# Mixer heads in halves of TensorE's rows or columns, in place of zero-filled operands

## The chip, the cores and the metric

One core of a Trainium2 chip runs the whole program. The metric is the device time of one execution in microseconds (us), the median of three runs. TensorE (PE) multiplies; VectorE (DVE) and ScalarE (ACT) do the elementwise work; SyncE (SP) issues the loads of weights.

## The reference, cut to what is computed

```python
for l in range(2):                      # h: 272 tokens (16 meta + 256) x 1024
    h += 0.5 * swiglu(rms(h), ffn1)     # 1024 -> 2816 -> 1024
    p = rms(h) @ w_in                   # 2688 columns, split over three head groups
    A = hgrn2(q, f, v, g)               # 6 heads of 64: gated linear recurrence, rms per head, gate
    B = sliding_window(q, k, v, sinks)  # 6 query heads, 2 key heads of 64, window 128, meta tokens
    C = conformer_conv(u)               # 256 channels, 31 taps, LayerNorm, swish
    h += concat(A, B, C) @ w_out
    h += 0.5 * swiglu(rms(h), ffn2)
return rms(h[:, 16:])
```

## The kernel before

Activations lie with channels on the 128 partitions and the 272 tokens along the free axis. Weights stream from HBM in 1 MB chunks; `Weights.split` makes of each a high part (ACT, L114) and a residual (DVE, L116), and every 128x128 weight tile is multiplied in three fp32r matmuls (L230 to L232). The fp32 matmuls of the mixer are run by the chip in two passes each, every pass with its own weight load.

A mixer is a row of projections, `proj(name, between, ...)`: 24 weight matmuls and then the small jobs in `between`, in the program's order on PE. ACT and DVE take theirs in an order that a scheduler writes down at build time. The jobs that the change touches:

- Recurrence (group A): the causal 272x272 matrix of each of 6 heads is built in levels b = 1, 2, 4, ... 64. `pairs(b)` multiplies keys `kk` (two heads of 64 channels share a 128-row tile) with the odd blocks of the queries. `stage(b)` copies those blocks into `qs`, per head into a half of its own, with the other head's rows zero: so one matmul over 128 rows gives both heads side by side, 128 columns wide (L470, and 16 wide for the last 16 tokens, L474). `keep(b)` copies the wanted places out of PSUM into `a0`, `a1`, `at`. `far` does the same for tokens 128 on (`ptl` L547, `pf` L552, from the zero-filled `qt` and `qs`).
- `outputs(i)`: values times matrix for the two heads of tile i, one after the other, three matmuls each (L601, L602, L603), head 0 into PSUM rows 0 to 63 and head 1 into 64 to 127. DVE adds the diagonal (L604), ACT squares (L605).
- `out_stats`: mean squares of the 6 heads with a 128x6 operand (`pr`, L611), root on ACT, reciprocal on DVE (L614). `out_norm(i)`: a 6x128 matmul spreads tile i's two factors over the partitions (`prb`, L618), one after each of three groups of output weights (`pw`); DVE multiplies (L619, L620) and splits into `y0h`, `y0l`.
- Attention (group B): `scores` puts a bf16 mask into PSUM (L659) and adds queries times keys (L661) per head; `bk` holds each key head with the other's rows zero. Then maximum (DVE L666), exp (ACT L671), normalisation (ACT L685, DVE L683), transposes (L697), and `values` (L729), in two column halves, one per key head.

Of the kernel before, what the change touches and what calls it, by code (L numbers as in the profile page):

```python
# [15 lines left out]
P = 128  # L16
# [121 lines left out]
def tile_hybrid_trunk(ctx: ExitStack, tc: tile.TileContext, hT: bass.AP, wst: bass.AP, par: bass.AP,  # L138
# [49 lines left out]
    for b in range(2):  # L188
        nc.gpsimd.memset(ones_q[b * 64:(b + 1) * 64, b * 64:(b + 1) * 64], 1.0)
    ident = cn[:, K_ID:K_ID + P]  # L190
# [166 lines left out]
    def mixer(l, nrm, t0, nxt):  # L357
# [16 lines left out]
        a0, a1, at = T([P, 6, N], "a0"), T([P, 6, 144], "a1"), T([META, 6, META], "at")  # L374
        qs = [T([P, 3, 2, 144], f"qs{i}") for i in range(2)]
        qt = T([P, 3, 2, META], "qt")
# [3 lines left out]
        bk = T([P, 2, N], "bk")  # L380
        for z in ([q[:, :, :t0]] if t0 else []) + [hc[:, :, :TAPS - 1], qs[0], qs[1], qt, bk, a0, a1, at]:
            nc.gpsimd.memset(z, 0.0)
# [73 lines left out]
        def stage(b):  # L456
            no = (N if b <= 8 else SEQ) // 2
            st = qs[levels.index(b) % 2]
            for hh in range(2):
                hs = slice(hh * 64, (hh + 1) * 64)  # L460
                nc.scalar.copy(st[hs, :, hh, :no].rearrange("p h (m b) -> p h m b", b=b),
                               odd(q[hs, :, :2 * no], b))

        def pairs(b):
            st = qs[levels.index(b) % 2]
            for g in range(2):
                ps = lev_ps[g] = bank(f"pl{b}_{g}_{l}")
                m = P if b < 64 else 64
                for i in range(3):
                    nc.tensor.matmul(ps[:m, i * P:(i + 1) * P], kk[:, i, g * P:g * P + m],  # L470
                                     st[:, i, :, g * 64:(g + 1) * 64], start=True, stop=True)
                if g == 1 and b <= 8:
                    for i in range(3):
                        nc.tensor.matmul(ps[:META, 384 + i * 16:384 + (i + 1) * 16], kk[:, i, SEQ:],  # L474
                                         st[:, i, :, 128:136], start=True, stop=True)

        def keep(b):
            lev = levels.index(b)
            for g, dst in enumerate((a0, a1)):
                ps = lev_ps[g]  # L480
# [13 lines left out]
            if b <= 8:  # L494
                shp = [META, 6, 8 // b, b]
                nc.vector.copy_predicated(
                    odd(at, b),
                    lv[:META, lev, :8].rearrange("p (m b) -> p m b", b=b).unsqueeze(1).broadcast_to(shp),
                    ps[:META, 384:432].rearrange("p (h m b) -> p h m b", h=6, b=b))
# [34 lines left out]
        def stage_far():  # L534
            tl = decay[128]
            st = qs[1]
            for hh in range(2):
                hs = slice(hh * 64, (hh + 1) * 64)
                nc.scalar.copy(qt[hs, :, hh, :], q[hs, :, SEQ:])
                nc.scalar.copy(st[hs, :, hh, :128], q[hs, :, 128:SEQ])  # L540
                nc.vector.tensor_tensor(st[hs, :, hh, 128:144], q[hs, :, SEQ:],
                                        tl[hs, :, 1:2].broadcast_to([64, 3, META]), op=ALU.mult)

        def far():
            ps = bank(f"ptl_{l}")
            for i in range(3):
                nc.tensor.matmul(ps[:, i * 32:(i + 1) * 32], kk[:, i, 128:SEQ],  # L547
                                 qt[:, i, :, :], start=True, stop=True)
            nc.scalar.copy(a1[:, :, 128:144], ps[:, :96].rearrange("p (h t) -> p h t", h=6))
            for i in range(3):  # L550
                ps = bank(f"pf{i}_{l}")
                nc.tensor.matmul(ps[:, :288], kk[:, i, :P], qs[1][:, i, :, :], start=True, stop=True)  # L552
                nc.scalar.copy(a0[:, 2 * i:2 * i + 2, 128:272],
                               ps[:, :288].rearrange("p (h t) -> p h t", h=2))
# [40 lines left out]
        def outputs(i):  # L595
            ps = bank(f"po{i}_{l}")
            for hh in range(2):
                hd = 2 * i + hh
                po = ps[hh * 64:(hh + 1) * 64, :]
                cs = slice(hd * 64, (hd + 1) * 64)  # L600
                nc.tensor.matmul(po[:, :N], vt[:, 0, cs], a0[:, hd, :], start=True, stop=False)  # L601
                nc.tensor.matmul(po[:, 128:272], vt[:, 1, cs], a1[:, hd, :], start=False, stop=False)  # L602
                nc.tensor.matmul(po[:, 256:272], vtt[:, cs], at[:, hd, :], start=False, stop=True)  # L603
            nc.vector.tensor_tensor(DG()[:, i, :], ps[:, :N], DG()[:, i, :], op=ALU.add)  # L604
            nc.scalar.activation(v[:, i, :], DG()[:, i, :], AF.Square)  # L605

        
        def out_stats():
            ps = bank(f"pr_{l}")
            for i in range(3):  # L610
                nc.tensor.matmul(ps[:6, :N], cn[:, K_B6 + 6 * i:K_B6 + 6 * i + 6], v[:, i, :], start=i == 0, stop=i == 2)  # L611
            rs = L([P, N], "rs", "rs")[:6, :]
            nc.scalar.activation(rs, ps[:6, :N], AF.Sqrt, bias=eps[:6])
            nc.vector.reciprocal(rs, rs)  # L614

        def out_norm(i):
            ps = bank(f"prb{i}_{l}")
            nc.tensor.matmul(ps[:, :N], cn[:6, K_S6 + i * P:K_S6 + (i + 1) * P], late["rs"][:6, :], start=True, stop=True)  # L618
# [12 lines left out]
        def keys(ps):  # L631
            for hh in range(2):
                hs = slice(hh * 64, (hh + 1) * 64)
                nc.vector.tensor_tensor(bk[hs, hh, :], ps[hs, :], r[hs, :], op=ALU.mult)

        class Heads:
# [3 lines left out]
            def __init__(self, name, groups, parts, lhs, prt, mask, nsk, kv):  # L640
                self.name, self.groups, self.parts, self.lhs, self.prt = name, groups, parts, lhs, prt
                self.mask, self.nsk, self.kv = mask, nsk, kv
                self.nk = sum(e - s for s, e in parts)
                self.per = 512 // self.nk
# [5 lines left out]
            def scores(self, g0):  # L650
                prt, nk = self.prt, self.nk
                ps = bank(f"ps{self.name}{g0}_{l}")
                g1 = min(self.groups, g0 + self.per)
                o = 0
                for gi in range(g0, g1):
                    mo = self.mask
                    for ks, ke in self.parts:
                        w = ke - ks
                        nc.tensor.matmul(ps[:prt, o:o + w], identb[:, :prt], conb[:, mo:mo + w],  # L659
                                         start=True, stop=False)  # L660
                        nc.tensor.matmul(ps[:prt, o:o + w], self.lhs(gi), bk[:, self.kv(gi), ks:ke],  # L661
                                         start=False, stop=True)
                        o += w
                        mo += w
                nm, nsk = self.nm[:, g0:g1], self.nsk[:prt, g0:g1]
                nc.vector.tensor_reduce(nm, ps[:prt, :o].rearrange("p (g k) -> p g k", g=g1 - g0),  # L666
                                        axis=AX.X, op=ALU.max)
                nc.vector.scalar_tensor_tensor(nm, nm, -SCALE, nsk, op0=ALU.mult, op1=ALU.min)
                for gi in range(g0, g1):
                    o = (gi - g0) * nk  # L670
                    nc.scalar.activation(self.p[:, gi, :], ps[:prt, o:o + nk], AF.Exp,  # L671
                                         bias=self.nm[:, gi:gi + 1], scale=SCALE,
                                         accum_out=self.den[:, gi:gi + 1])
# [29 lines left out]
        h0 = Heads("0", 6, [(0, 128)], lambda g: BQ()[:, g % 3, :P], P, K_M0, nsink[:, sk:sk + 6], lambda g: g // 3)  # L703
        h1 = Heads("1", 6, [(0, 256)], lambda g: BQ()[:, g % 3, P:SEQ], P, K_M1, nsink[:, sk:sk + 6], lambda g: g // 3)
        ht = Heads("t", 2, [(0, META), (P, N)], lambda g: bqt, 48, K_MT, nsinkt[:, 2 * l:2 * l + 2], lambda g: g)
# [16 lines left out]
        def values(hd, parts, sl):  # L722
            def go():
                ps = bank(f"pv{hd.name}_{l}")
                w = hd.groups * hd.prt // 2
                for kvh in range(2):
                    hs = slice(kvh * 64, (kvh + 1) * 64)
                    for pi, (off, kn, vsrc) in enumerate(parts):
                        nc.tensor.matmul(ps[hs, :w], vsrc[:kn, hs], pt[hd.name, off][:kn, kvh * w:(kvh + 1) * w],  # L729
                                         start=pi == 0, stop=pi == len(parts) - 1)  # L730
# [48 lines left out]
        proj("bv", [level(8, 1), lambda: h0.scores(0), lambda: h0.scores(4), lambda: h1.scores(0)], scaled(bv))  # L779
        proj("v0", [level(16, 1), bv_rows, lambda: h1.scores(2), lambda: h1.scores(4), h0.soft], scaled(v[:, 0, :]))  # L780
# [166 lines left out]
```

## Time and profile before

| | |
|---|---|
| median of 3 runs (lowest to highest) | 1061.64 us (1060.98 to 1061.72) |
| the profiled execution: time, span | 1060.9 us, 1059.1 us |
| TensorE's granted clock, whole span | 0.997 of full speed |
| busy share of the span: PE, DVE, ACT | 98%, 70%, 53% |
| mixer of layer 0, of layer 1 (by the places of their instructions) | about 212 to 338 us, 737 to 864 us |

A busy share counts overlapping instructions once. PE's matmuls are pipelined and their ends modelled, so a busy PE may still contain gaps, and the time of a small job is read from start to start, as the chain of waits gives it, and not from the duration of its instructions. All places below are in the mixer of layer 0; layer 1 repeats them.

### The profile page before, as it was taken

How to read it: one execution, taken by the hardware profiler on the slowest of the kernel's cores; microseconds unless marked ns; L12 is line 12 of the kernel's file. 1: busy time of each engine (PE TensorE's matmuls, PEld its weight loads, DVE VectorE, ACT ScalarE, POOL GpSimd, SP SyncE). 2: the span in 40 equal slices, each digit the busy share in tenths (PEclk: the TensorE clock that was granted, in tenths of full speed). 3: DMA queues.
4: the chain of work that ended last, by engine and by line, in shares of the span. 5: the costliest groups of instructions: out<-in, count | busy, mean ns of one | idle time of the engine just before them, and what ended most of it. 6: DMA issues, size and time to landing. Idle time of an engine off the chain costs nothing.

```text
span 1059.1 us, 19879 instructions
## 1 busy us (share of the span) xinstructions
PE 1043.0 (98%) x8324; PEld 1020.2 (96%) x8324; DVE 746.6 (70%) x1225; ACT 557.4 (53%) x879; POOL 13.1 (1%) x33
## 2 busy tenths in 40 slices
PE   7999999999999999999999999999999999999996
PEld 7999999999879999999999999999998799999996
DVE  7876655589968777665566766555999688767552
ACT  7644444454847644444454444444668466554441
POOL 0000000110000000000000000001000000000000
PEclk9999999999999999999999999999999999999998
DMA  8554554554214454544545454454422245545521
GB/s 313 223 189 168 178 180 166 194 176 151 79 52 152 168 199 160 189 169 174 185 162 195 162 182 178 162 187 169 174 106 83 78 162 196 197 166 196 181 98 40
DMA packets 27433, 173.08 MB, mean 163 GB/s; under 512 B 2832, under 2 KB 6032, under 8 KB 7120
## 3 DMA queue, kind: packets, MB, share of 16 engines
q1 hardware_dynamic: 26208, 170.85, 45.1%
q8 instruction: 65, 1.06, 0.4%
q10 hardware_dynamic: 1056, 0.52, 0.2%
q0 software_dynamic: 80, 0.44, 0.1%
q14 instruction: 24, 0.20, 0.1%
HBM read 170.76 MB, written 1.05 MB: 162 GB/s over the span
## 4 chain that ended last, share of the span: by engine, by line
PE 98%; DVE 1%; DMA 0%; SPq 0%; ACT 0%; issue 0%; DVEq 0%
PE pd_f L231 8%; PE pd_f L232 8%; PE pd_f L230 8%; PE pg_f L230 8%; PE pu_f L230 8%; PE pu_f L231 8%; PE pg_f L231 8%; PE pu_f L232 8%; PE pg_f L232 8%; PE pl L470 2%; PE pw L230 1%; PE pw L231 1%; PE pw L232 1%; PE ps L661 1%; PE po L601 1%; PE pp_g L230 1%
## 5 line engine op out<-in xcount | busy, mean ns | idle before, releaser
L114 ACT CAST wh<-raw 128x1024 fp32r<-128x1024 f32 (+1 forms) x324 | 336.1, 1040 | 369.9 <-PE pu_f L231 118.4
L116 DVE TENSOR_TENSOR wl<-raw,wh 128x1024 fp32r<-128x1024 f32 (+1 forms) x328 | 393.2, 1202 | 144.4 <-ACT wh L114 143.6
L231 PE MATMUL pd_f<-ml_f,wh 128*128 128x272 f32 (+1 forms) x704 | 202.7, 288 | 0.0
L232 PE MATMUL pd_f<-mh_f,wl 128*128 128x272 f32 (+1 forms) x704 | 201.7, 286 | 0.0
L230 PE MATMUL pd_f<-mh_f,wh 128*128 128x272 f32 (+1 forms) x704 | 201.2, 286 | 0.0
L230 PE MATMUL pg_f<-xh,wh 128*128 128x272 f32 (+1 forms) x672 | 192.7, 287 | 0.1
L230 PE MATMUL pu_f<-xh,wh 128*128 128x272 f32 (+1 forms) x672 | 192.5, 286 | 0.0
L231 PE MATMUL pu_f<-xl,wh 128*128 128x272 f32 (+1 forms) x672 | 192.5, 286 | 0.0
L232 PE MATMUL pg_f<-xh,wl 128*128 128x272 f32 (+1 forms) x672 | 192.5, 286 | 0.0
L231 PE MATMUL pg_f<-xl,wh 128*128 128x272 f32 (+1 forms) x672 | 192.5, 286 | 0.0
L232 PE MATMUL pu_f<-xh,wl 128*128 128x272 f32 (+1 forms) x672 | 192.5, 286 | 0.0
L230 PEld LDWEIGHTS pd_f<-mh_f,wh 128*128 128x128 f32 x704 | 132.6, 188 | 0.0
L232 PEld LDWEIGHTS pd_f<-mh_f,wl 128*128 128x128 f32 x704 | 132.3, 188 | 0.0
L231 PEld LDWEIGHTS pd_f<-ml_f,wh 128*128 128x128 f32 x704 | 132.2, 188 | 0.0
L230 PEld LDWEIGHTS pg_f<-xh,wh 128*128 128x128 f32 x672 | 126.3, 188 | 0.5 <-PE pu_f L232 0.3
L232 PEld LDWEIGHTS pg_f<-xh,wl 128*128 128x128 f32 x672 | 126.3, 188 | 0.0
L230 PEld LDWEIGHTS pu_f<-xh,wh 128*128 128x128 f32 x672 | 126.3, 188 | 0.0
L231 PEld LDWEIGHTS pu_f<-xl,wh 128*128 128x128 f32 x672 | 126.3, 188 | 0.0
L231 PEld LDWEIGHTS pg_f<-xl,wh 128*128 128x128 f32 x672 | 126.3, 188 | 0.0
L232 PEld LDWEIGHTS pu_f<-xh,wl 128*128 128x128 f32 x672 | 126.3, 188 | 0.0
L321 DVE TENSOR_TENSOR u_f<-pu_f,r 128x272 f32<-128x272 f32 (+1 forms) x88 | 38.1, 435 | 50.8 <-PE pu_f L232 50.6
L319 DVE TENSOR_TENSOR g_f<-pg_f,r 128x272 f32<-128x272 f32 (+1 forms) x88 | 38.0, 435 | 26.5 <-PE pg_f L232 26.5
(297 smaller groups left out, 1490.3 us busy)
## 6 DMA issues: line engine op xcount, KB each, us to landing
raw<-wst SPq DMA_DIRECT2D x158, 1024.0 KB, 4.8
raw<-wst SPq DMA_DIRECT2D x5, 512.0 KB, 7.3
h<-hT SPq DMA_DIRECT2D x3, 272.0 KB, 4.8
raw<-wst SPq DMA_DIRECT2D x2, 256.0 KB, 4.1
out<-h SPq DMA_DIRECT2D x2, 256.0 KB, 2.3
out<-h ACTq DMA_DIRECT2D x2, 256.0 KB, 2.5
msk<-msk POOLq DMA_DIRECT2D x1, 432.0 KB, 3.5
h<-hT SPq DMA_DIRECT2D x2, 136.0 KB, 2.9
```

What stands on the lines that cost most here:

```text
L114: self.nc.scalar.copy(h[:, s], raw)
L116: self.nc.vector.tensor_tensor(lo[:, s], raw, h[:, s].bitcast(F32), op=ALU.subtract)
L230: nc.tensor.matmul(back(ps), wh, back(ah), start=first, stop=False)
L231: nc.tensor.matmul(back(ps), wh, back(al), start=False, stop=False)
L232: nc.tensor.matmul(back(ps), wl, back(ah), start=False, stop=last)
L319: nc.vector.tensor_tensor(g, pss[0][:, :n], r[:, s], op=ALU.mult)
L321: nc.vector.tensor_tensor(u, pss[1][:, :n], r[:, s], op=ALU.mult)
L470: nc.tensor.matmul(ps[:m, i * P:(i + 1) * P], kk[:, i, g * P:g * P + m], st[:, i, :, g * 64:(g + 1) * 64], start=True, stop=True)
L601: nc.tensor.matmul(po[:, :N], vt[:, 0, cs], a0[:, hd, :], start=True, stop=False)
L661: nc.tensor.matmul(ps[:prt, o:o + w], self.lhs(gi), bk[:, self.kv(gi), ks:ke], start=False, stop=True)
```

## The change

The two heads of a tile become two matmuls, one in rows 0 to 63 of TensorE's array and one in rows 64 to 127 (`kk[hs]`, `st[hs]`), which alternate and write two different PSUM banks: in `pairs`, `far` and `scores`. In `outputs` and `values` the two heads alternate in column halves, as the order of loops is turned. `out_stats` uses three column groups of 32 and `out_norm` three row groups of 32, its three matmuls issued together. `qs`, `qt` and `bk` have no zero-filled part any more, `a0` and `a1` become one tile `aa`. The mask goes in with one matmul per bank, and all scores of `h1` move from the slot after `bv` to the slot after `v0`. Two new constants, `stat_w` and `back_w` (the latter by three small DMAs on POOL's queue), take 640 bytes of each partition, and what is placed behind them moves by as much. Weights, the number of weight matmuls and the FFNs are as they were.

```diff
         def stage(b):
...
-            for hh in range(2):
-                hs = slice(hh * 64, (hh + 1) * 64)
-                nc.scalar.copy(st[hs, :, hh, :no].rearrange("p h (m b) -> p h m b", b=b),
-                               odd(q[hs, :, :2 * no], b))
+            nc.scalar.copy(st[:, :, :no].rearrange("p h (m b) -> p h m b", b=b), odd(q[:, :, :2 * no], b))
         def pairs(b):
...
-                    nc.tensor.matmul(ps[:m, i * P:(i + 1) * P], kk[:, i, g * P:g * P + m],
-                                     st[:, i, :, g * 64:(g + 1) * 64], start=True, stop=True)
+                    for hh in range(2):
+                        hs, o = slice(hh * 64, (hh + 1) * 64), (3 * g + i) * 64
+                        nc.tensor.matmul(lev_ps[hh][:m, o:o + 64], kk[hs, i, g * P:g * P + m],
+                                         st[hs, i, g * 64:(g + 1) * 64], start=True, stop=True)
...
         def outputs(i):
...
+            for step in range(3):
+                for hh in range(2):
...
+                    if step == 0:
+                        nc.tensor.matmul(po[:, :N], vt[:, 0, cs], aa[:, hh, 0, i, :], start=True, stop=False)
...
         def out_stats():
             ps = bank(f"pr_{l}")
             for i in range(3):
-                nc.tensor.matmul(ps[:6, :N], cn[:, K_B6 + 6 * i:K_B6 + 6 * i + 6], v[:, i, :], start=i == 0, stop=i == 2)
+                nc.tensor.matmul(ps[32 * i:32 * (i + 1), :N], stat_w, v[:, i, :], start=True, stop=True)
...
         def out_norm(i):
-            ps = bank(f"prb{i}_{l}")
-            nc.tensor.matmul(ps[:, :N], cn[:6, K_S6 + i * P:K_S6 + (i + 1) * P], late["rs"][:6, :], start=True, stop=True)
+            if i == 0:
+                for x in range(3):
+                    spread[x] = bank(f"prb{x}_{l}")
+                    xs = slice(32 * x, 32 * (x + 1))
+                    nc.tensor.matmul(spread[x][:, :N], back_w[xs, :], late["rs"][xs, :], start=True, stop=True)
+            ps = spread[i]
...
-            def scores(self, g0):
+            def scores(self, *gs):
...
+                for ps in pss:
+                    nc.tensor.matmul(ps[:prt, :len(gs) * nk].rearrange("p (g k) -> p g k", k=nk), identb[:, :prt],
+                                     conb[:, self.mask:self.mask + nk].unsqueeze(1).broadcast_to([P, len(gs), nk]),
+                                     start=True, stop=False)
+                for x, g in enumerate(gs):
...
+                        for kv, ps in enumerate(pss):
+                            rows = slice(kv * 64, (kv + 1) * 64)
+                            nc.tensor.matmul(ps[:prt, o:o + ke - ks], self.lhs(g)[rows], bk[rows, ks:ke],
+                                             start=False, stop=x == len(gs) - 1 and ke == self.parts[-1][1])
...
-        proj("bv", [level(8, 1), lambda: h0.scores(0), lambda: h0.scores(4), lambda: h1.scores(0)], scaled(bv))
-        proj("v0", [level(16, 1), bv_rows, lambda: h1.scores(2), lambda: h1.scores(4), h0.soft], scaled(v[:, 0, :]))
+        proj("bv", [level(8, 1), lambda: h0.scores(0, 1, 2)], scaled(bv))
+        proj("v0", [level(16, 1), bv_rows, lambda: h1.scores(0, 1), lambda: h1.scores(2), h0.soft], scaled(v[:, 0, :]))
```

How the instructions stand on PE at two of these places, of before and of the change (a row: line, operation, result<-inputs, partitions x elements of the result; xN repeats it). First level 1 in layer 0, the tile `pl` in its two banks, with the first tails, before:

```order
L470 MATMUL pl_0_0_2891<-qs_0_2418,kk_2425 128x128 x3
L470 MATMUL pl_1_0_2895<-qs_0_2418,kk_2425 128x128 x3
L474 MATMUL pl_1_0_2895<-qs_0_2418,kk_2425 16x16 x3
```

and in the change:

```order
L480 MATMUL pl_0_0_2891<-qs_0_2426,kk_2432 128x64
L480 MATMUL pl_1_0_2892<-qs_0_2426,kk_2432 128x64
L480 MATMUL pl_0_0_2891<-qs_0_2426,kk_2432 128x64
L480 MATMUL pl_1_0_2892<-qs_0_2426,kk_2432 128x64
L480 MATMUL pl_0_0_2891<-qs_0_2426,kk_2432 128x64
L480 MATMUL pl_1_0_2892<-qs_0_2426,kk_2432 128x64
...
L486 MATMUL pl_0_0_2891<-qs_0_2426,kk_2432 16x8
L486 MATMUL pl_1_0_2892<-qs_0_2426,kk_2432 16x8
```

Six matmuls of 128 columns have become twelve of 64 that alternate between two banks, and three tails six.

Then `outputs(0)` on PE, head 0 and head 1, before:

```order
L601 MATMUL po_0_3497<-a_0_2415,vt_2458 64x272
L602 MATMUL po_0_3497<-a_0_2416,vt_2458 64x144
L603 MATMUL po_0_3497<-at_2417,vtt_2459 64x16
L601 MATMUL po_0_3497<-a_0_2415,vt_2458 64x272
L602 MATMUL po_0_3497<-a_0_2416,vt_2458 64x144
L603 MATMUL po_0_3497<-at_2417,vtt_2459 64x16
```

and in the change:

```order
L614 MATMUL po_0_3547<-aa_2424,vt_2460 64x272 x2
L616 MATMUL po_0_3547<-aa_2424,vt_2460 64x144 x2
L618 MATMUL po_0_3547<-at_2425,vtt_2461 64x16 x2
```

The same six matmuls now stand in three pairs, each a step of both heads.

## Rows read from the trace of the kernel before

**Rows 1.** The page, part 4: the chain that ended last, by engine.
```profile
PE 98%; DVE 1%; DMA 0%; SPq 0%; ACT 0%; issue 0%; DVEq 0%
```

**Rows 2.** PE's waits in the mixers: who for, us in total, times, longest.
```profile
PE pw L231 <- DVE y0l L248: 0.3, 1, 0.3
```

**Rows 3.** Windows of 10 us: span, then busy PE, PEld, DVE, ACT, POOL, clock, DMA.
```profile
250.00:260.00 10.00, 10.00 (x94) 9.54 (x93) 10.00 (x22) 4.96 (x9) 0.00 (x0) 1.00 0.29 107
270.00:280.00 10.00, 10.00 (x86) 9.33 (x85) 8.94 (x27) 9.79 (x31) 0.00 (x0) 1.00 0.16 45
```

**Rows 4.** The chain of waits around level 1: start us, us, what.
```profile
243.98 0.12 PE pp_bq L232
244.11 1.34 PE pl L470 x12
245.44 0.25 PE pl L474 x6
```

**Rows 5.** The chain at `out_norm(0)`, and at `out_stats`.
```profile
311.16 0.65 PE prb L618 x2
311.81 0.32 PE pw L230
...
304.97 1.47 PE pr L611 x6
```

**Rows 6.** The chain at level 64 and at `far`.
```profile
278.47 1.45 PE pl L470 x12
...
284.37 0.59 PE ptl L547 x6
284.96 1.54 PE pf L552 x6
```

**Rows 7.** The chain in the scores of `h0`, and of `h1`.
```profile
260.43 0.06 PE ps L659
260.49 0.28 PE ps L661 x2
...
268.37 0.11 PE ps L659
268.48 0.43 PE ps L661 x2
```

**Rows 8.** Timeline of PE and of its weight loads at `values(h0)`: start us, us, what.
```profile
286.43 0.87 PE L729 MATMUL pv<-pt,bvt 128*64 128x384 f32 x4
287.22 0.50 PE L577 MATMUL pdg<-qk,ones_q 128*128 128x272 f32 x1
...
286.43 0.20 PEld L729 LDWEIGHTS pv<-pt,bvt 128*64 128x64 f32 x4 [0.39 <-issue]
```

**Rows 9.** The chain from `values(ht)` to one head of `outputs(0)`.
```profile
295.33 1.22 PE pvt L729 x12
296.55 0.60 PE po L601 x2
297.15 0.24 PE po L602 x2
297.39 0.21 PE po L603 x2
```

**Rows 10.** Tile `po`: line, engine, count, ns min/median/max, first and last start.
```profile
L601 PEld LDWEIGHTS po<-a,vt x24: 132/134/136, 296.5 to 825.8; 128*64 128x64 f32 x24
L603 PEld LDWEIGHTS po<-at,vtt x24: 127/130/131, 297.3 to 826.7; 16*64 16x64 f32 x24
```

**Rows 11.** Timeline of DVE after `po1` and after `prb2`: start us, us, what [idle before].
```profile
300.82 0.44 DVE L604 TENSOR_TENSOR dg<-po,dg 128x272 f32<-128x272 f32 x1 [1.27 <-PE po L603]
315.79 0.44 DVE L619 TENSOR_TENSOR dg<-prb,dg 128x272 f32<-128x272 f32 x1 [0.71 <-PE prb L618]
```

**Rows 12.** Busy time by windows, PE alone, in weight products of the FFNs.
```profile
160.00:205.00 45.00, 45.00 (x364) 1.00 0.52 184
480.00:530.00 50.00, 50.00 (x401) 1.00 0.48 172
```

More of the change, by code (lines that the diff above doesn't have):

```diff
@@ L189, in tile_hybrid_trunk @@
         nc.gpsimd.memset(ones_q[b * 64:(b + 1) * 64, b * 64:(b + 1) * 64], 1.0)
+    stat_w = const.tile([P, 32], F32, name="stat_w")
+    nc.gpsimd.memset(stat_w, 0.0)
+    for b in range(2):
+        nc.gpsimd.memset(stat_w[b * 64:(b + 1) * 64, b:b + 1], 1.0 / 64)
+    back_w = const.tile([96, P], F32, name="back_w")
+    nc.gpsimd.memset(back_w, 0.0)
+    for i in range(3):
+        nc.gpsimd.dma_start(back_w[32 * i:32 * i + 2, :], con[0:2, K_S6:K_S6 + P])
     ident = cn[:, K_ID:K_ID + P]
@@ L372, in Y @@
             return [y[:, k - 3 * g, :] for y in ys[g]]
-        a0, a1, at = T([P, 6, N], "a0"), T([P, 6, 144], "a1"), T([META, 6, META], "at")
-        qs = [T([P, 3, 2, 144], f"qs{i}") for i in range(2)]
-        qt = T([P, 3, 2, META], "qt")
+        aa, at = T([P, 2, 2, 3, N], "aa"), T([META, 2, 3, META], "at")
+        qs = [T([P, 3, 272], f"qs{i}")[:, :, :144] for i in range(2)]
         hc = T([P, 2, N + TAPS - 1], "hc")
@@ L379, in mixer @@
         f, kk, q = T([P, 3, N], "f"), T([P, 3, N], "kk"), T([P, 3, N], "q")
-        bk = T([P, 2, N], "bk")
-        for z in ([q[:, :, :t0]] if t0 else []) + [hc[:, :, :TAPS - 1], qs[0], qs[1], qt, bk, a0, a1, at]:
+        bk = T([P, N], "bk")
+        for z in ([q[:, :, :t0]] if t0 else []) + [hc[:, :, :TAPS - 1], aa, at]:
             nc.gpsimd.memset(z, 0.0)
@@ L458, in stage @@
             st = qs[levels.index(b) % 2]
-            for hh in range(2):
-                hs = slice(hh * 64, (hh + 1) * 64)
-                nc.scalar.copy(st[hs, :, hh, :no].rearrange("p h (m b) -> p h m b", b=b),
-                               odd(q[hs, :, :2 * no], b))
+            nc.scalar.copy(st[:, :, :no].rearrange("p h (m b) -> p h m b", b=b), odd(q[:, :, :2 * no], b))
         def pairs(b):
             st = qs[levels.index(b) % 2]
+            lev_ps.update({hh: bank(f"pl{b}_{hh}_{l}") for hh in range(2)})
+            m = P if b < 64 else 64
             for g in range(2):
-                ps = lev_ps[g] = bank(f"pl{b}_{g}_{l}")
-                m = P if b < 64 else 64
                 for i in range(3):
-                    nc.tensor.matmul(ps[:m, i * P:(i + 1) * P], kk[:, i, g * P:g * P + m],
-                                     st[:, i, :, g * 64:(g + 1) * 64], start=True, stop=True)
[L472 to L475, printed above, removed]
+                    for hh in range(2):
+                        hs, o = slice(hh * 64, (hh + 1) * 64), (3 * g + i) * 64
+                        nc.tensor.matmul(lev_ps[hh][:m, o:o + 64], kk[hs, i, g * P:g * P + m],
+                                         st[hs, i, g * 64:(g + 1) * 64], start=True, stop=True)
+            if b <= 8:
+                for i in range(3):
+                    for hh in range(2):
+                        hs, o = slice(hh * 64, (hh + 1) * 64), 384 + i * 8
+                        nc.tensor.matmul(lev_ps[hh][:META, o:o + 8], kk[hs, i, SEQ:],
+                                         st[hs, i, 128:136], start=True, stop=True)
         def keep(b):
             lev = levels.index(b)
-            for g, dst in enumerate((a0, a1)):
-                ps = lev_ps[g]
+            for hh in range(2):
+                ps = lev_ps[hh]
+                dst = aa[:, hh].rearrange("p g i n -> p (g i) n")
                 if b == 32:
@@ L493, in keep @@
                     nc.scalar.copy(dst[:64, :, 64:128], ps[:64, :384].rearrange("p (h t) -> p h t", h=6))
[L494 to L499, printed above, removed]
+                if b <= 8:
+                    shp = [META, 3, 8 // b, b]
+                    nc.vector.copy_predicated(
+                        odd(at[:, hh], b),
+                        lv[:META, lev, :8].rearrange("p (m b) -> p m b", b=b).unsqueeze(1).broadcast_to(shp),
+                        ps[:META, 384:408].rearrange("p (h m b) -> p h m b", h=3, b=b))
         def views(b):
@@ L534, in stage_far @@
         def stage_far():
-            tl = decay[128]
-            st = qs[1]
-            for hh in range(2):
[L538 to L554, printed above, removed]
+            tl, st = decay[128], qs[1]
@@ new lines, in stage_far, with far @@
+            nc.scalar.copy(st[:, :, :128], q[:, :, 128:SEQ])
+            nc.vector.tensor_tensor(st[:, :, 128:144], q[:, :, SEQ:],
+                                    tl[:, :, 1:2].broadcast_to([P, 3, META]), op=ALU.mult)
+        def far():
+            pss = [bank(f"pf{hh}_{l}") for hh in range(2)]
+            for i in range(3):
+                for hh in range(2):
+                    hs = slice(hh * 64, (hh + 1) * 64)
+                    nc.tensor.matmul(pss[hh][:, i * 144:(i + 1) * 144], kk[hs, i, :P], qs[1][hs, i, :],
+                                     start=True, stop=True)
+            for i in range(3):
+                for hh in range(2):
+                    hs, o = slice(hh * 64, (hh + 1) * 64), 432 + i * META
+                    nc.tensor.matmul(pss[hh][:, o:o + META], kk[hs, i, P:SEQ], q[hs, i, SEQ:],
+                                     start=True, stop=True)
+            for hh in range(2):
+                nc.scalar.copy(aa[:, hh, 0, :, 128:272], pss[hh][:, :432].rearrange("p (h t) -> p h t", h=3))
+                nc.scalar.copy(aa[:, hh, 1, :, 128:144], pss[hh][:, 432:480].rearrange("p (h t) -> p h t", h=3))
@@ L596, in outputs @@
             ps = bank(f"po{i}_{l}")
[L597 to L603, printed above, removed]
+            for step in range(3):
+                for hh in range(2):
+                    po, cs = ps[hh * 64:(hh + 1) * 64, :], slice((2 * i + hh) * 64, (2 * i + hh + 1) * 64)
+                    if step == 0:
+                        nc.tensor.matmul(po[:, :N], vt[:, 0, cs], aa[:, hh, 0, i, :], start=True, stop=False)
+                    elif step == 1:
+                        nc.tensor.matmul(po[:, 128:272], vt[:, 1, cs], aa[:, hh, 1, i, :144], start=False, stop=False)
+                    else:
+                        nc.tensor.matmul(po[:, 256:272], vtt[:, cs], at[:, hh, i, :], start=False, stop=True)
             nc.vector.tensor_tensor(DG()[:, i, :], ps[:, :N], DG()[:, i, :], op=ALU.add)
@@ L610, in out_stats @@
             for i in range(3):
-                nc.tensor.matmul(ps[:6, :N], cn[:, K_B6 + 6 * i:K_B6 + 6 * i + 6], v[:, i, :], start=i == 0, stop=i == 2)
-            rs = L([P, N], "rs", "rs")[:6, :]
-            nc.scalar.activation(rs, ps[:6, :N], AF.Sqrt, bias=eps[:6])
+                nc.tensor.matmul(ps[32 * i:32 * (i + 1), :N], stat_w, v[:, i, :], start=True, stop=True)
+            rs = L([P, N], "rs", "rs")[:96, :]
+            nc.scalar.activation(rs, ps[:96, :N], AF.Sqrt, bias=eps[:96])
             nc.vector.reciprocal(rs, rs)
+        spread = {}
         def out_norm(i):
-            ps = bank(f"prb{i}_{l}")
-            nc.tensor.matmul(ps[:, :N], cn[:6, K_S6 + i * P:K_S6 + (i + 1) * P], late["rs"][:6, :], start=True, stop=True)
+            if i == 0:
[4 more added lines that the diff above has]
+            ps = spread[i]
             nc.vector.tensor_tensor(DG()[:, i, :], ps[:, :N], DG()[:, i, :], op=ALU.mult)
@@ L631, in keys, with __init__ @@
         def keys(ps):
-            for hh in range(2):
-                hs = slice(hh * 64, (hh + 1) * 64)
-                nc.vector.tensor_tensor(bk[hs, hh, :], ps[hs, :], r[hs, :], op=ALU.mult)
+            nc.vector.tensor_tensor(bk, ps, r, op=ALU.mult)
         class Heads:
-            def __init__(self, name, groups, parts, lhs, prt, mask, nsk, kv):
+            def __init__(self, name, groups, parts, lhs, prt, mask, nsk):
                 self.name, self.groups, self.parts, self.lhs, self.prt = name, groups, parts, lhs, prt
-                self.mask, self.nsk, self.kv = mask, nsk, kv
+                self.mask, self.nsk = mask, nsk
                 self.nk = sum(e - s for s, e in parts)
-                self.per = 512 // self.nk
                 self.p = T([prt, groups, self.nk], f"pex{name}")
@@ L648, in __init__ @@
                 self.es = T([prt, groups], f"es{name}")
-            def scores(self, g0):
[L651 to L656, printed above, removed]
-                    for ks, ke in self.parts:
[L658 to L673, printed above, removed]
@@ new lines, in scores @@
+            def scores(self, *gs):
+                prt, nk, half = self.prt, self.nk, self.groups // 2
+                pss = [bank(f"ps{self.name}{gs[0]}_{kv}_{l}") for kv in range(2)]
+                for ps in pss:
[3 more added lines that the diff above has]
+                for x, g in enumerate(gs):
+                    o = x * nk
+                    for ks, ke in self.parts:
+                        for kv, ps in enumerate(pss):
+                            rows = slice(kv * 64, (kv + 1) * 64)
+                            nc.tensor.matmul(ps[:prt, o:o + ke - ks], self.lhs(g)[rows], bk[rows, ks:ke],
+                                             start=False, stop=x == len(gs) - 1 and ke == self.parts[-1][1])
+                        o += ke - ks
+                for kv, ps in enumerate(pss):
+                    g0 = kv * half + gs[0]
+                    g1 = g0 + len(gs)
+                    nm, nsk = self.nm[:, g0:g1], self.nsk[:prt, g0:g1]
+                    nc.vector.tensor_reduce(nm, ps[:prt, :len(gs) * nk].rearrange("p (g k) -> p g k", k=nk),
+                                            axis=AX.X, op=ALU.max)
+                    nc.vector.scalar_tensor_tensor(nm, nm, -SCALE, nsk, op0=ALU.mult, op1=ALU.min)
+                    for gi in range(g0, g1):
+                        o = (gi - g0) * nk
+                        nc.scalar.activation(self.p[:, gi, :], ps[:prt, o:o + nk], AF.Exp,
+                                             bias=self.nm[:, gi:gi + 1], scale=SCALE,
+                                             accum_out=self.den[:, gi:gi + 1])
@@ L702, in mixer @@
         sk = 6 * l
-        h0 = Heads("0", 6, [(0, 128)], lambda g: BQ()[:, g % 3, :P], P, K_M0, nsink[:, sk:sk + 6], lambda g: g // 3)
-        h1 = Heads("1", 6, [(0, 256)], lambda g: BQ()[:, g % 3, P:SEQ], P, K_M1, nsink[:, sk:sk + 6], lambda g: g // 3)
-        ht = Heads("t", 2, [(0, META), (P, N)], lambda g: bqt, 48, K_MT, nsinkt[:, 2 * l:2 * l + 2], lambda g: g)
+        h0 = Heads("0", 6, [(0, 128)], lambda g: BQ()[:, g, :P], P, K_M0, nsink[:, sk:sk + 6])
+        h1 = Heads("1", 6, [(0, 256)], lambda g: BQ()[:, g, P:SEQ], P, K_M1, nsink[:, sk:sk + 6])
+        ht = Heads("t", 2, [(0, META), (P, N)], lambda g: bqt, 48, K_MT, nsinkt[:, 2 * l:2 * l + 2])
         pt = {}
@@ L725, in go @@
                 w = hd.groups * hd.prt // 2
-                for kvh in range(2):
-                    hs = slice(kvh * 64, (kvh + 1) * 64)
-                    for pi, (off, kn, vsrc) in enumerate(parts):
+                for pi, (off, kn, vsrc) in enumerate(parts):
+                    for kvh in range(2):
+                        hs = slice(kvh * 64, (kvh + 1) * 64)
                         nc.tensor.matmul(ps[hs, :w], vsrc[:kn, hs], pt[hd.name, off][:kn, kvh * w:(kvh + 1) * w],
```

## The prediction

> **What bounds the kernel now.** I read the chain of waits first: 98% of the span is PE [rows 1], so a microsecond that PE no longer needs in a mixer is one off the time, unless PE then waits. Next PE's waits by releaser: in the mixers it waits for another engine 0.3 us in all [rows 2], at the output weights. Third the windows, to see who is near PE: DVE is busy for 10.00 of 10 us in one stretch of the mixer and ACT for 9.79 in another, at a granted clock of 1.00 [rows 3], so faster work there may be met by a late engine. Last the chain around each job that changes. It gives times from start to start, with nothing counted twice.
>
> Three readings carry the sum. (a) A pass of 128 columns takes 0.112 us (1.34 over 12) [rows 4], one of only 32 takes 0.098 (0.59 over 6) [rows 6]. A quarter of the columns is hardly cheaper: with 128 weight columns the load bounds short passes. (b) Going into an array split and out of it costs something. The matmul after `prb` takes 0.32 us [rows 5] where such a one takes 0.12 [rows 4], so 0.20 out. In: `prb` takes 0.65 for 2 passes of 272; from the unsplit passes of 288 at 1.54 over 6 [rows 6], two of 272 are 0.49, which leaves 0.16; from `pr` with 1.47 for 6 passes [rows 5], four passes more are 0.82, a pass 0.205, which leaves 0.24. I take 0.2. (c) Two column halves run together: four passes of 384 at `values(h0)` take 0.79 us (286.43 to 287.22), and their four weight loads lie within 0.20 [rows 8], where a single one takes 0.13 [rows 10]. One after the other the passes would take 4 x 384/288 x 0.257 = 1.37.
>
> **The change part by part, for one layer; plus is time saved.**
>
> Pairs. At each level 12 matmuls of 64 columns (24 passes) take the place of 6 of 128 (12 passes). If two row halves go together there are 12 pairs of passes, and by (a) a pair still costs 0.098 to 0.112, since the load bounds it: 1.34 again, no gain. Levels 1 to 8 pay one more split going in, 0.2 each; their tails run in a split already and pay the way out now. They become 6 pairs for 6 passes, and I leave the 0.25 [rows 4] as it is. Level 16 is followed by unsplit transposes and pays in and out, 0.4; level 32 is followed by scores in a split of 48 weight columns and pays 0.2. Level 64 has only 64 weight columns, so both load and stream halve: from 1.45 [rows 6] to (1.45 - 0.2)/2 + 0.2 = 0.83, plus 0.6; the bounds are 0 and that. Together -0.8 - 0.4 - 0.2 + 0.6 = **-0.8**.
>
> Scores. `h0` takes 6 x (0.06 + 0.28) = 2.04 [rows 7]. Then the masks cost the same columns, 0.36, three pairs 3 x 0.28 = 0.84, one split in and out 0.4: 1.60, plus 0.4. `h1` takes 6 x (0.11 + 0.43) = 3.24 [rows 7]; then 0.66 + 3 x 0.43 + two splits 0.8 = 2.75, plus 0.5. **+0.9**; the small tail scores at nothing.
>
> `far`. 0.59 + 1.54 = 2.13 [rows 6] becomes six pairs of 144 columns at 0.128 (half of 0.257), six load-bound pairs 0.59 and a split in 0.2; the column halves of the values behind it pay the way out already. 1.56, **+0.6**.
>
> `values(ht)`. Twelve passes in 1.22 [rows 9], of which kv 0 and kv 1 now alternate. Between 0 and half of it; **+0.5**. The values of `h0` and `h1` overlap already by (c): nothing.
>
> `outputs`. A head takes 0.60 + 0.24 + 0.21 = 1.05, and because the third step stands between the heads, six of them are serial: 6.3 [rows 9]. Alternating as in (c), a tile takes a head's time: 3.15 saved. At the ratio of (c), 0.79/1.37 = 0.58, it is 6.3 x 0.42 = 2.65; but that 0.79 holds a split and a first load which the 1.05 holds too, so I take **+3.1**.
>
> `out_stats`. 1.47 for three matmuls in a row [rows 5] becomes one triple: a third and a split, 0.49 + 0.2: **+0.8**, between 0 and 1.
>
> `out_norm`. Three times 0.65 + 0.20 [rows 5] becomes once: **+1.7**; it needs the row groups of 32 to go together, else it keeps two splits' worth, 2 x 0.4 = 0.8.
>
> Other engines. ACT copies `qs` in one piece for two. DVE loses one multiply of `keys`, gains four small copies of `at` and some per-bank maxima, about a microsecond in a stretch where it is full [rows 3]; PE saves little before that stretch ends, so it needs nothing sooner. That cover is thin later. At `outputs` DVE idles 1.27 us per tile [rows 11]; a tile will take PE 1.05 less, so DVE just keeps up. At `out_norm` PE is 1.7 sooner at the weights that need `y0l`, where it waits 0.3 today; DVE regains at least the 0.71 it idled for the last `prb` [rows 11]. The wait that comes is between nothing and 1.3 (0.3 + 1.7 - 0.71); I take **-0.5**. The three DMAs for `back_w` run at the start on POOL's queue, and their first reader stands near 311 us [rows 5]; they hold up nobody. All loads of weights keep their place.
>
> Sum: -0.8 + 0.9 + 0.6 + 0.5 + 3.1 + 0.8 + 1.7 - 0.5 = 6.3 per layer, 12.6 for two. The profiled execution took 1060.9, 0.7 below the median of 1061.64, so 1048.3 against the one and 1049.0 against the other: I say **1048.5**.
>
> **The rivals.**
>
> *Row halves don't load together (slower).* No instruction of this trace uses rows from 64 on alone; (c) shows only columns. If the weight loads of two row halves go one after the other, each pair costs 0.224 instead of 0.112: 12 x 0.112 = 1.34 at each of six levels, 8.1; level 64 loses its 0.6, `h0` 0.7, `far` 0.6 + 6 x (0.224 - 0.128) = 1.2. That is 10.6 per layer against a gain of 6.3, 8.6 slower over two: **1070**. It decides from a pair's price of about 0.18 (0.112 x (1 + 6.3/10.6)). Against it: the four loads of the column halves within 0.20. For it: nothing but that no row shows it. Chance 0.13. The Trainium skill, "TensorEngine Tiling (Array Packing)", Key Properties, says that different tiles can load weights and multiply in parallel, rows or columns; rows 8 agree for columns, and no run here shows it for rows. By that rule this rival is out and the forecast stands.
>
> *DVE becomes the bound (smaller gain).* If `dg`, the squares or `y0l` come late, the reciprocal, `pr` or the output weights wait: the full 1.3 at `y0l` in place of 0.5, and up to 1.3 at `outputs`, where DVE's idle time is used up [rows 11]: 2.1 per layer, 4.2 in all, **1052.7**. Likewise ACT at 9.79 of 10 [rows 3], now that all scores of `h1` come in one slot and their normalisation follows later. Chance 0.14.
>
> *Loads halve as well (larger gain).* If 64 rows load in half the time, a pair costs some 0.06, the levels save 0.67 each six times, `h0` and `far` 0.3 each: 4.6 per layer, **1039**. Rows 10 speak against it: a load of 16 rows takes 130 ns, one of 128 rows 134. Chance 0.03. The Trainium skill, same page, Theoretical Speedup, gives up to 2x where the contracted dimension is at most 64; on the pairs that would be this case. The rows 4 and 6 rather say that such passes are bound by a load that no halving shortens.
>
> *Places in memory.* The operands of the weight stream move by 640 bytes. Like products run at 45/364 = 123.6 ns in one FFN and 50/401 = 124.7 in another [rows 12], where only the place of an operand differs; 0.9% of the some 960 us that lie outside the changed jobs would be 9 us either way, **1057** or **1040**. Against it: all of them move together, and their distances are kept. Chance 0.05, half of it in each direction.
>
> **How the numbers follow.** Forecast 0.65, row halves serial 0.13, DVE or ACT 0.14, halved loads 0.03, places 0.05. The forecast's own range, from the bounds of `outputs` (0.45), `values(ht)`, level 64 and the wait (some 0.6 each), two layers, is 1045 to 1052. From 1044.5 to 1054.5 it takes in DVE: 0.65 + 0.14, less a little for the tails of both, is near 0.8. A change of up to 0.2%, 2.1 us, can't be told from none. Slower: 0.13 and a little for places, 0.14. Same: mixtures of the cases, among them places that give the gain back, 0.03. Faster: the rest, 0.83.
>
> **What would show it.** Right: `pl` at 1.3 to 1.6 us per level, `po` at about 1.05 per tile, `pr` near 0.7, one group of `prb` of about 0.65, PE's waits for DVE under 2 us in all, weight matmuls at their old spacing. Wrong: `pl` at 2.6 (loads serial), weight loads of the two halves that start 0.1 apart and not some 10 ns, long waits of PE for `dg`, `v` or `y0l`, or another spacing in the FFNs.

## The result, and the profile after

The changed kernel takes 1047.31 us (1046.66 to 1047.70, 4 runs) against 1061.31 (1060.50 to 1061.72): a ratio of 0.9869, 95% interval 0.9857 to 0.9880, or 14.0 us less. Forecast were 1048.5, between 1044.5 and 1054.5.

First PE's matmuls of the norms (`pn`, one group for each norm; that of an FFN stands among its first products), of before and then of the change, from the timelines. The first and second bracket the mixer of layer 0, the fourth and fifth that of layer 1; two FFNs lie between the second and the fourth.

```profile
213.82 0.29 PE L297 MATMUL pn<-ah,ones_r 128*128 128x272 f32 x1
354.08 0.29 PE L297 MATMUL pn<-ah,ones_r 128*128 128x272 f32 x1
...
738.73 0.29 PE L297 MATMUL pn<-ah,ones_r 128*128 128x272 f32 x1
876.61 0.28 PE L297 MATMUL pn<-ah,ones_r 128*128 128x256 f32 x1
```

```profile
215.12 0.29 PE L306 MATMUL pn<-ah,ones_r 128*128 128x272 f32 x1
348.11 0.29 PE L306 MATMUL pn<-ah,ones_r 128*128 128x272 f32 x1
...
732.74 0.29 PE L306 MATMUL pn<-ah,ones_r 128*128 128x272 f32 x1
863.42 0.28 PE L306 MATMUL pn<-ah,ones_r 128*128 128x256 f32 x1
```

Measured from `pn` to `pn`, the mixers fall from 140.26 to 132.99 and from 137.88 to 130.68 us: 7.27 and 7.20, 14.5 together. The FFNs between take 384.65 and 384.63: moving all operands by 640 bytes did nothing. Before the first mixer the changed run is 1.3 later (215.12 against 213.82), of which more below. So the whole gain is in the mixers, and it is the same in both.

Now the chain of waits of the change, in layer 1: level 1, a tile of outputs, the statistics and the spread.

```profile
762.58 1.49 PE pl L480 x24
764.07 0.24 PE pl L486 x12
764.31 0.32 PE pp_bq L239
...
813.00 0.61 PE po L614 x4
813.61 0.24 PE po L616 x4
813.85 0.22 PE po L618 x4
...
818.21 0.59 PE pr L626 x6
...
823.29 0.66 PE prb L638 x6
823.95 0.32 PE pw L239
```

Four passes of `po` now take 0.61, as two did [rows 9]: two heads cost what one cost. Six passes of `prb` take 0.66, as two did, and `pr` 0.59 for 1.47 [rows 5]. But `pl` takes 1.49 for 24 passes against 1.34 for 12 [rows 4]: the halves run together, and it isn't faster.

That they do is seen in the timeline of level 1, loads and matmuls:

```profile
245.33 1.42 PEld L480 LDWEIGHTS pl<-qs,kk 64*128 64x128 f32 x24
245.33 1.55 PE L480 MATMUL pl<-qs,kk 64*128 64x64 f32 x24
```

24 loads lie in 1.42 us, 0.059 each, where an unsplit pass needs 0.112 for one. Loads that take half as long, one after the other, would look the same; e6 below excludes them, since there 24 passes with one row half at a time take 2.43 us, 0.10 each.

PE's waits after:

```profile
PE pg_f L249 <- ACT wh L114: 6.0, 1, 6.0
PE pg_f L249 <- ACT xh L273: 1.7, 1, 1.7
PE pn L309 <- ACT q L287: 0.7, 1, 0.7
PE pw L240 <- DVE y0l L257: 0.3, 1, 0.3
```

The wait for `y0l` has not grown [rows 2]. A new stop is in the chain instead, ahead of the transposes of `h1`'s last weights (`pt`):

```profile
287.25 1.14 DVE wl L116
288.39 0.82 DVE cv L433 x2
289.21 0.36 DVE dg L591
289.57 0.04 issue
289.62 0.96 PE pt L720 x6
```

The nine transposes of `v` start at 288.35 and take 0.98 us where nothing stops them, so PE is through at 289.33; it starts `pt` at 289.62, released by `dg`: `far` takes two PSUM banks fewer than before, so `pt` gets a bank that the diagonal used, which VectorE empties late because convolution taps (`cv`, each one multiplication and addition of the 31 of a channel) and a weight residual (`wl`) stand in front. That `far` and the rotation of the banks are the reason is read from the program; that the late `dg` is what `pt` waits for is in the chain. With a second short stop inside `pt`, this costs about 0.5 us per layer. The list of waits leaves it out here and shows 0.2 of it in e1, so short stops are read from the starts and not from the list.

### The profile page after: what moved, and what is told of

It is laid out like the page before. It is cut to its first block, busy times and chain, and to the rows that moved or that the text cites. A ratio compares the mean times of both kernels' runs of the same rounds, so it can differ in the third digit from the quotient of the medians.

```text
span 1045.9 us, 20317 instructions
## 1 busy us (share of the span) xinstructions
PE 1028.4 (98%) x8548; PEld 1008.0 (96%) x8548; DVE 744.9 (71%) x1237; ACT 546.8 (52%) x859; POOL 13.4 (1%) x30
## 4 chain that ended last, share of the span: by engine, by line
PE 69%; DVE 3%; ACT 1%; issue 0%; DVEq 0%; ACTq 0%
PE pd_f L240 6%; PE pd_f L241 6%; PE pd_f L239 6%; PE pg_f L239 6%; PE pu_f L239 6%; PE pu_f L241 6%; PE pu_f L240 6%; PE pg_f L240 6%; PE pg_f L241 6%; PE pw L240 2%; PE pw L241 1%; PE pw L239 1%; DVE cv L433 1%; PE pl L480 1%; DVE wl L116 1%; PE pp_g L239 0%
```

## The experiments

Mixer lengths are from `pn` to `pn` as above; ratios are to the kernel before on the same chip. The change, e1 and e2 have the same mixers, and their lengths agree within 0.02 us; so tenths of a microsecond in these lengths count, where the ratios can't tell runs apart.

| run | ratio (95%) | mixer 0, mixer 1 (us) |
|---|---|---|
| e1 changed again | 0.9861 (0.9845 to 0.9878) | 133.01, 130.68 |
| e2 late back_w | 0.9861 (0.9846 to 0.9875) | 133.01, 130.68 |
| e3 diagonal last | 0.9862 (0.9848 to 0.9877) | 133.19, 130.54 |
| e4 both | 0.9863 (0.9848 to 0.9877) | 133.20, 130.54 |
| e5 outputs in turn | 0.9929 (0.9913 to 0.9945) | 136.16, 133.84 |
| e6 pairs in turn | 1.0013 (0.9999 to 1.0027) | 140.14, 139.33 |
| e7 spread apart | 0.9899 (0.9884 to 0.9915) | 134.69, 132.36 |
| e8 zero-filled levels | 0.9862 (0.9846 to 0.9879) | 133.28, 130.15 |
| e9 taps held | 0.9859 (0.9844 to 0.9874) | 133.37, 129.98 |
| e10 taps on GpSimd | 0.9897 (0.9880 to 0.9913) | 135.24, 131.87 |
| e11 zero-filled, GpSimd | 0.9900 (0.9885 to 0.9914) | 134.29, 132.54 |
| e12 zero-filled, held | 0.9842 (0.9828 to 0.9855) | 132.32, 129.21 |

**The start.** The theory was that the three small loads of `back_w` cost the 1.3 us.

> The changed kernel once more, unaltered, as the base for the three beside it on the same chip. Near 0.987 of the kernel before, some 14.0 us faster. Theory: the first matmul group of the first FFN again waits some 1.7 us for the scaled input (0.7 before), because the three small loads of back_w stand in front of pieces of the first weight chunk; its first norm matmul again starts near 29.7 us (28.4 before). Rival: that was chance of one profile, and it starts near 28.4 this time.

> The memset of back_w and its three small loads move from the start of the program to the start of the first mixer, behind the load of the masks. Theory (the small loads delay the first weights): the first norm matmul starts near 28.4 us, and the time falls by 1.0 to 1.3 us against the changed kernel run beside it, to about 1046. Rival (chance, or the places of the tiles in memory): no change, within 0.5 us, and the start stays at 29.7.

The unaltered kernel had its first norm matmul at 28.59 us this time, as early as before. The theory falls: the start differs from run to run. e2 settles nothing of itself, since the scheduler put the loads where they had been, at 2.13 us:

```profile
2.13 1.67 POOL L212 DMA_DIRECT2D back_w<-con  x3
```

**Undoing single parts.** Outputs, the loops turned back:

```diff
-            for step in range(3):
-                for hh in range(2):
+            for hh in range(2):
+                for step in range(3):
```

> Undoes one part: in the outputs all three steps of head 0 come before those of head 1, as before the change; the rest stays. Theory (the gain there is two column halves that run together, which the third step in between prevented): the three tiles take 6.4 us per layer instead of 3.2, and the time rises by 6 us, to about 1053. Rival (the engine looks far enough ahead to pair them itself, or VectorE sets the pace there anyway): less than 2 us.

The mixers are 3.17 and 3.16 us longer than in the change; the three tiles take 6.37 instead of 3.22. The alternation itself is the gain. The same for the spread:

```diff
-            if i == 0:
-                for x in range(3):
...
+            spread[i] = bank(f"prb{i}_{l}")
+            xs = slice(32 * i, 32 * (i + 1))
```

> The three spreading matmuls of the head factors go back to three places, one after each of three groups of output weights, still in row groups of 32. Theory (three array splits become one): each place costs 0.65 and 0.2 behind it, so 1.7 us more per layer, 3.4 in all, less what the shorter wait for y0l gives back (at most 0.3 per layer): near 1050. Rival (VectorE behind them is the bound): under 1 us.

The mixers are 1.70 and 1.68 longer: as forecast, and VectorE gave nothing back (the wait for `y0l` is 0.3 as before). Then the alternation of row halves at the levels:

```diff
-            for g in range(2):
-                for i in range(3):
-                    for hh in range(2):
+            for hh in range(2):
+                for g in range(2):
+                    for i in range(3):
```

> At the levels all six matmuls of head 0 come before the six of head 1, so that row halves no longer alternate; the rest stays. Theory (24 passes hide in the time of 12 only because two row halves load and multiply together): a level takes 12 more loads of 0.112 us, 2.8 instead of 1.5 us, level 64 0.6 more; 8.7 us per layer, 17 in all, some of it hidden where the engine would have waited for VectorE: 1062 to 1064, the whole gain lost. Rival (loads are pulled ahead over the six matmuls of a head): under 3 us.

The whole gain is gone. The chain around level 4, and the granted clock (the number after PE's busy time and count) in windows:

```profile
255.81 2.43 PE pl L480 x24
258.24 0.24 PE pl L486 x12
258.48 0.32 PE pp_bv L239
...
259.07 0.23 PE pp_bv L239
```

```profile
250.00:258.00 8.00, 8.00 (x84) 1.00 0.37 133
258.00:260.00 2.00, 2.00 (x23) 0.73 0.00 0
260.00:262.00 2.00, 2.00 (x10) 0.50 0.00 0
262.00:264.00 2.00, 2.00 (x17) 0.92 0.00 0
```

24 passes take 2.43 us for 1.49: 0.94 more at six levels and 0.51 at the last, 6.15 per layer. Unforeseen is the rest: behind level 4 the granted clock goes to 0.50, the 1.2 GHz level, and weight matmuls take 0.23 for 0.12 for a while, some 15 of them, 1.5 us. Layer 1 lost about 3 in the same way, behind levels 8 and 32 (0.58 from 788 to 792 us, 0.63 from 804 to 808). Less the 0.5 of the stop at the diagonal, which is gone here, that is the 7.15 and 8.65 by which its mixers are longer than those of the change.

**What the levels are worth.** Levels 1 to 32 zero-filled again, `aa` laid out as group, head, tile:

```diff
+                for i in range(3):
+                    nc.tensor.matmul(to[:, i], kk[:, i, g * P:g * P + P],
+                                     st[:, i, :, g * 64:(g + 1) * 64], start=True, stop=True)
```

> Levels 1 to 32 go back to one matmul over 128 rows with zero-filled queries, both heads side by side; level 64 and all else stay in halves. Theory (such passes are bound by the load of 128 weight columns, so halves save nothing there and each level pays a split): TensorE is 0.06 us faster at levels 1 to 8, 0.15 to 0.35 at levels 16 and 32, some 0.6 per layer, 1.2 in all; ScalarE copies twice as often there, VectorE has four small copies less. Between 1045 and 1048. Rival (the rows in halves are worth something of themselves): 2 us or more slower than the changed kernel.

From `pn` to the transposes of `v` TensorE needs 72.2 us for the change's 73.2, and in layer 1 71.4 for 72.4: halves cost 1.0 per layer at these levels. The time doesn't show it, since PE then waits longer at the same place:

```profile
PE pt L732 <- DVE y1l L770: 1.2, 1, 1.2
PE pt L732 <- DVE dg L603: 0.9, 1, 0.9
```

**The stop at the diagonal.** In e3 the transposes go ahead of the diagonal.

```diff
-lambda: diagonal(0), lambda: diagonal(1), lambda: diagonal(2), v_rows, rows(h1, P, P), conv(3)]
+v_rows, rows(h1, P, P), lambda: diagonal(0), lambda: diagonal(1), lambda: diagonal(2), conv(3)]
```

> In the slot after g0 the three diagonal matmuls go behind the transposes of v and of the last part of h1's weights. Theory (far uses two banks fewer, so the banks of these transposes are now those of the diagonal, which the busy VectorE frees late): the 0.8 us that the six transposes take fall to 0.57 and the 0.3 us gap ahead of them goes, 0.5 us per layer and 1.0 us in all. Rival (VectorE itself is behind and the wait only moves to the next job that needs it): the six transposes are quick, but as much is waited at the values, the outputs or the next gate, and the time stays within 0.3 us.

> Both edits together, late loads of back_w and the diagonal last. If both theories hold, the gains add: 2.0 to 2.3 us below the changed kernel, near 1045. If only one holds, 1.0 to 1.3 below.

The rival holds: the mixers of e3 are 0.2 longer and 0.1 shorter than those of the change. `pt` no longer waits, and PE's waits have a new row, behind ScalarE, whose gate function now stood late because VectorE was late:

```profile
PE pvt L752 <- ACT ptt L722: 0.4, 1, 0.4
```

e9 leaves that order and holds five taps behind the diagonal (`held[0]` is the diagonal's last multiplication). In the trace of the change VectorE does 14 taps between 279 us and the diagonal, in e9 9 are left there:

```diff
-        proj("v2", [level(64, 2), rows(h0, 0, P), rows(h1, 0, P), ht.soft, conv(2)], scaled(v[:, 2, :]))
+        proj("v2", [level(64, 2), rows(h0, 0, P), rows(h1, 0, P), ht.soft, conv(14)], scaled(v[:, 2, :]))
...
+                with tc.issue_after(held[0]):
+                    conv(n)()
```

> The changed kernel, but five convolution taps that VectorE did ahead of the diagonal are held behind it. Theory (between the levels and the head statistics VectorE is full, so that work moved there only moves the wait): the six transposes of h1's weights take 0.57 us again and the gap ahead of them is gone, 0.5 us per layer, but the taps now stand ahead of the reciprocal of the head statistics and the spreading matmuls wait instead; the time within 1 us of the changed kernel. Rival (only the order was wrong, VectorE has room behind): the gain stays, 1.0 us in all, ratio near 0.9855.

The stop is gone (`pvt` 0.98, `pt` 0.57), layer 0 is 0.4 longer, layer 1 0.7 shorter: nothing clear in all. In layer 0 0.9 us are lost later. Nothing waits at the reciprocal or at the spread, where I had expected it. The first 0.36 are lost just behind the spread, where weights wait for `dg`, VectorE's first multiplication there, which has a tap and a weight residual in front of it:

```profile
307.75 0.36 DVE dg L649
308.12 0.04 issue
308.16 0.40 PE pw L239
```

The rest is spread over the convolution's statistics (0.3) and the first products of the FFN (0.2).

> As the run before it, and the last six taps of one channel tile are done on GpSimd (one multiply and one addition each) and added in with one addition: VectorE does 2.0 us less per layer. Theory (VectorE's sum of work is the bound there): the transposes are quick and nothing waits later: 0.5 us per layer, 1.0 in all, ratio near 0.985 to 0.9855 against 0.9861 to 0.9869 of the changed kernel. Rival (something else than VectorE's work sets the pace, or the two engines slow each other): the same as the changed kernel or slower, VectorE's taps longer than 0.42 us while GpSimd works.

> Zero-filled levels 1 to 32 together with the taps on GpSimd and seven taps held. Theory (the levels' 0.9 us per layer was lost only because VectorE came late): both gains add, 0.5 + 0.9 per layer, 2.8 in all: ratio near 0.9835 to 0.984, the fastest of all. Rival (ScalarE, which copies the queries twice as often, or VectorE is still late): at the six transposes or at the nine of v a wait stays, ratio 0.985 or more.

Both miss. GpSimd (POOL in the rows) takes 1.45 us for a multiplication and 1.16 for an addition on average, VectorE's taps in mixer 0 rise from 495 to 535 ns on average, and the queries of level 1 come late:

```profile
PE pl L495 <- ACT qs L483: 2.5, 2, 1.3
```

```profile
L429 POOL TENSOR_SCALAR cq<-hc,pr 128x272 f32<-128x272 f32 x10 | 14.5, 1447 | 0.8
L430 POOL TENSOR_TENSOR cp<-cp,cq 128x272 f32<-128x272 f32 x10 | 11.6, 1157 | 0.8
```

The rise is in the taps that run beside GpSimd's operations (225.4 to 240.3 us): these 12 take 690 ns on average, the other 42 491. Behind that wait the granted clock falls again (0.52 from 248 to 250 us). From the start of level 2 to the convolution's mean e10 takes 60.16 us, the changed kernel 60.68: the 0.5 us is there, and more is lost at level 1. Last, e8 and e9 together:

> Zero-filled levels 1 to 32 together with five taps held behind the diagonal, all on VectorE again. Theory (TensorE and VectorE are tied in the mixer from the diagonal to the mean of the convolution): TensorE reaches the diagonal some 0.9 us per layer earlier, but the taps come no sooner, so most of that is waited for at the diagonal's readers or at the mean: ratio 0.985 to 0.987, no clear gain over the changed kernel. Rival (the 0.9 us of the zero-filled levels are kept, as the holding removes the wait that ate them): 1.8 us less, ratio near 0.984.

Here the rival wins and my theory of a tie falls: 132.32 and 129.21 us, 2.1 less than the change, at 1044.63 (1043.76 to 1045.30). The list of PE's waits has none in the mixers any more:

```profile
PE pg_f L249 <- ACT wh L114: 5.9, 1, 5.9
PE pg_f L249 <- ACT xh L273: 1.7, 1, 1.7
PE pn L309 <- ACT q L287: 0.7, 1, 0.7
```

The starts say the same of layer 0: the nine transposes take 0.99 and `pt` 0.57.

```profile
286.44 1.15 PE L619 MATMUL pvt<-cn,v 128*128 128x128 f32 x9
287.43 0.82 PE L741 MATMUL pt<-cn,pex 128*128 128x128 f32 x6
288.00 0.37 PE L239 MATMUL pp_g<-xh,wh 128*128 128x272 f32 x1
```

In layer 1 `pt` still takes 0.79, so 0.2 of the stop is left there, and layer 0 loses the same 0.36 behind the spread as in e9. Against e8, which has the same work in another order, both mixers are 0.95 shorter. So it was the order of taps at one place, not VectorE's sum of work, that ate most of what the zero-filled levels gain. This version has the lowest ratio of all runs. Its interval, 0.9828 to 0.9855, lies just under that of the change (0.9857 to 0.9880), but it overlaps that of e1 (0.9845 to 0.9878); the gain over the change rests on the lengths of the mixers.

## Why the prediction was right, point by point

*Time and sign.* 14.0 us, against 12.6 by the sum and 13.1 by the stated time, in the range and with the mechanism that was forecast. Per layer, 7.2 to 7.3 came where 6.3 was expected; of the 0.9 more, 0.5 are in the pairs and 0.4 in the scores. The times below are from the first start of a job to that of the next.

*Pairs, forecast -0.8.* Shown in kind by e8 and e6: halves hide a second set of passes, and save nothing where 128 weight columns are loaded. The size is -0.3: in layer 0 levels 1 to 8 cost 0.15 each (1.67 to 1.73 us, and 0.1 at the weights ahead of them), levels 16 and 32 with the transposes between them 0.26 together, and level 64 gives 0.61 (1.46 to 0.85), as forecast. The term that was too dear is the split, taken at 0.2 going in and at 0.2 going out: levels 1 to 32 cost 0.9 where 1.4 was forecast. e8 prices the same levels at 1.0 within the changed kernel.

*Outputs +3.1, spread +1.7.* Measured 3.15 (6.37 to 3.22) and, undone singly, 3.2 and 1.7. *Statistics +0.8*: 0.88. *`values(ht)` +0.5*: 1.22 to 0.74. *`far` +0.6*: 2.21 to 1.51, with 0.1 given back at the weights ahead of it. *Scores +0.9*: 4.89 to 3.85; and the tail scores, put at nothing, gave 0.24. Less the stop of 0.55 these sum to 7.2.

*The wait, -0.5 at `y0l`.* The size was right by luck, the place was wrong. `y0l` waits 0.3 as before; the 0.5 arose at the transposes behind the diagonal. I had read VectorE as nearly full up to 280 us [rows 3], and so it is at the diagonal (9.90 us of those from 280 to 290, before), but wrote that PE "saves little before that stretch ends, so it needs nothing sooner": I did not follow which banks become free when `far` takes two fewer.

*Rivals.* Serial row halves: excluded by 24 loads in 1.42 us together with e6. What they cost e6 shows for the levels alone, 0.10 us per pass: 1060.75 against 1059.75, where I had given 8.6 us over before, with scores and `far` serial too and 0.112 per pass. Halved loads: excluded, `pl` did not fall. Places in memory: 384.65 and 384.63. VectorE as the bound: in part, as above.

## What to carry to other kernels

Splitting the array paid here for passes that are bound by what streams (`outputs`, statistics, spread) and for serial small jobs that can share one split; where a pass is bound by its 128 weight columns, zero-filled operands in a full array were as fast and spared the splits. Two tiles ran together only where their matmuls alternate in the program (e5, e6). After such a gain look at which bank or operand the next job gets: zero-filled levels alone (e8) shorten the two mixers by 0.2 us in all, five held VectorE operations alone (e9) by 0.3, both together (e12) by 2.1.

## What was not expected of the hardware

The granted clock can fall to half behind a stretch in which the engine was busy all along but with one row half at a time (0.50 from 260 to 262 us in e6), and weight matmuls then take 0.23 us for 0.12. And VectorE's taps took 690 ns beside GpSimd's operations, and 491 without them, in the same mixer (e10).
